# The sample's state updates in a hybrid decoder step: as row tiles of TensorE, four at a time

## The chip, the cores and the metric

The kernel runs on one core of one Trainium2 chip. The metric is the device time of one execution in microseconds; several executions are taken and their median is given. The core has five engines that run side by side, each with its own queue of instructions: TensorE (PE in the profile; its weight loads are PEld), VectorE (DVE), ScalarE (ACT), GpSimd (POOL) and SyncE (SP), which here only issues transfers. Matrix products land in PSUM, of which the kernel uses eight banks of 512 fp32 columns, four in each of the pools `mm` and `gl`; everything else lives in SBUF.

## What is computed

The kernel is one inference step of a two-layer decoder on two groups: a prompt (one sequence of 256 new positions) and a sample (eight sequences with eight new tokens each, which carry a state). Layer 0 mixes tokens by gated linear attention (GLA) with 4 heads, 256 key and 512 value dimensions each; layer 1 is a gMLP. Each layer is followed by a dense MLP of width 8192. All is fp32. The change is in the GLA. For one head, with the running sum b of the log decays:

```python
q_dec = qi * jnp.exp(b); k_inv = ki * jnp.exp(-b); k_to_end = ki * jnp.exp(b_last - b)
scores = jnp.where(causal, jnp.einsum('bhtk,bhsk->bhts', q_dec, k_inv), 0.0)
o = jnp.einsum('bhtk,bhkv->bhtv', q_dec, s) + jnp.einsum('bhts,bhsv->bhtv', scores, vi)
s_new = (jnp.exp(b_last[..., 0, :])[..., None] * s
         + jnp.einsum('bhsk,bhsv->bhkv', k_to_end, vi))
```

For the sample, s is an input of 256x512 for each of 8 sequences and 4 heads, and both o and s_new are needed. The product in s_new contracts over only 8 tokens.

## The kernel before

The 256 prompt positions and the 64 sample tokens stand together as 320 columns. A weight matrix of 2048 rows is read in units of 512 rows by 256 columns (0.5 MB, `unit`, L129). ScalarE rounds a unit to fp32r (`wh`, L144), VectorE takes the rest, which it splits off (`wl`, L145), and TensorE runs three matmuls of 320 columns for each 128x128 piece (`mm3`, L161 to L163), 24 for a unit (two halves of the columns, four pieces of the rows, three each), into PSUM banks of the pool `mm`. Raw weights have three buffers and the split ones four. This makes up nearly all of the time in both layers.

The attention's small work is laid between the units: `Side` (L60) holds a list of steps and gives out about as many after each unit as are left per unit. The steps of a head (`steps`, L629) are spread over the 8 units of its own r projection and the 8 of the next head's k and q projection; the last head has only 8 and 2. Behind that list a scheduler sets the final order on each engine by priority, its own estimate of when operands are ready, and the buffers of the pools. Each engine then works its queue strictly in order.

The steps of a head: the sample's scores, then `sample_first` (L580), which starts the sample's output in one bank `po` of the pool `gl` (four banks); it stays there until the last sample step. Then come five prompt steps (scores, two outputs, two states) with two sample steps after each, and the other sample steps. There are 16 sample steps in a head, one for each of 8 sequences and each half `kt` of the keys (`sample_step`, L589). Each splits 128x512 of the state into `sth` (ScalarE, L597) and `stl` (VectorE, L598), adds two matmuls to `po` (L600), and makes one update matmul (L603) with which VectorE updates the state (L604). After the second half GpSimd's queue stores the sequence's state (L607). States are loaded two sequences ahead (`load`, L577), into four buffers `st` (pool `g3`), which also serve the inputs at the kernel's start.

The eight tokens of a sequence stand in 32 rows: values as high and low part twice (`vts`), keys as high, high, low, low (`kst`, L411 to L416), so that a contraction over 32 rows gives the product of the split parts. Four sequences share the 128 rows of a tile. The update of one of them contracts over all 128 rows, with keys from `kz`, where the other three have zeros in place of keys:

```python
nc.tensor.matmul(pu[:], kz[:, g, i, kt * P : (kt + 1) * P], hd.vts[:, g, :], start=True, stop=True)
nc.vector.scalar_tensor_tensor(st[:, kt, :], st[:, kt, :], hd.dec[...], pu[:], op0=ALU.mult, op1=ALU.add)
```

`kz` is cleared once (L284) and filled by four copies of 32 rows for each half of the keys of a head (L427 to L431).

The prompt's scores (`prompt_scores`, L514) are matmuls with 64 output columns of the array, which TensorE runs in tiles of 128x64, two beside each other.

Of the kernel before, what the change touches and what calls it, by code (L numbers as in the profile page):

```python
# [8 lines left out]
F32 = mybir.dt.float32  # L9
F32R = mybir.dt.float32r  # L10
I32 = mybir.dt.int32
AF = mybir.ActivationFunctionType
ALU = mybir.AluOpType
AX = mybir.AxisListType

P = 128
D = 2048
KT = D // P
TP = 256
DB, DS = 8, 8  # L20
# [3 lines left out]
DK, DV = 256, 512  # L24
CH = 64
NCH = TP // CH
# [51 lines left out]
def step_kernel(ctx: ExitStack, tc: tile.TileContext, A):  # L78
    nc = tc.nc
    uid = [0]  # L80

    def nm(s):
        uid[0] += 1
        return f"{s}_{uid[0]}"
# [16 lines left out]
    def mmtile(n=T):  # L101

        if mx is not None:
            banks[0] = (banks[0] + 1) % 6
        return (mx if banks[0] > 3 else mm).tile([P, n], F32, tag="mm", name=nm("mm"), padded_shape=[P, 512])

    def gltile(n=512):
        return gl.tile([P, n], F32, tag="gl", name=nm("gl"), padded_shape=[P, 512])
# [16 lines left out]
    def col(c):  # L125
        return vec[:, c : c + 1]
# [86 lines left out]
    gst = ExitStack()  # L213
    gp = gst.enter_context(tc.tile_pool(name="gp", bufs=1))
    g2 = gst.enter_context(tc.tile_pool(name="g2", bufs=2))
    g3 = gst.enter_context(tc.tile_pool(name="g3", bufs=4))


    xT = A["xT"].rearrange("(k p) t -> p k t", p=P)
# [59 lines left out]
    fac = gp.tile([P, 2, 9], F32, tag="fac", name="fac")  # L279
    nc.vector.memset(fac[:], 1.0)  # L280


    kz = gp.tile([P, 2, 4, DK], F32R, tag="kz", name="kz")
    nc.gpsimd.memset(kz[:].bitcast(F32), 0.0)  # L284

    glow = gp.tile([96, T], F32R, tag="glow", name="glow")

    wgr = gp.tile([P, 2, TP], F32, tag="sq", name="wgr")[:, 0, :].rearrange("p (k n) -> p k n", n=16)
# [33 lines left out]
    SO = A["o_state_s"]  # L322

    def bc4(ap):

        return ap.rearrange("p (b o t) -> p b o t", b=DB, o=1)

    def chunks(ap):
        return ap.rearrange("p (n w) -> p n w", w=CH)

    class Head:
# [6 lines left out]
        def tiles(hd):  # L338
            hd.qd = gp.tile([P, 2, T], F32, tag="qd", name=nm("qd"))
            hd.qx = gp.tile([P, 2, 5 * CH], F32, tag="qx", name=nm("qx"))  # L340
            hd.kip = gp.tile([P, 2, TP], F32, tag="kip", name=nm("kip"))
            hd.kte = gp.tile([P, 2, T], F32, tag="kte", name=nm("kte"))
            hd.kis = gp.tile([P, 2, DB, 4, DS], F32, tag="kis", name=nm("kis"))
            hd.ktp = gp.tile([P, 2, DK], F32, tag="ktp", name=nm("ktp"))
            hd.vtp = gp.tile([P, 2, DV], F32, tag="vtp", name=nm("vtp"))
            hd.vts = gp.tile([P, 2, DV], F32R, tag="vts", name=nm("vts"))

        def gate_logits(hd):

            hd.dec = g2.tile([P, 2, NCH + DB], F32, tag="dec", name=nm("dec"))  # L350
            for kt in range(2):
                hd.eb[kt] = g2.tile([P, T], F32, tag="eb", name=nm("eb"))
                hd.ei[kt] = g2.tile([P, T], F32, tag="ei", name=nm("ei"))
                f = 2 * hd.h + kt
                ps = gltile(T)
                nc.tensor.matmul(ps[:], wg2[:, f * P : (f + 1) * P], glow[:], start=True, stop=True)
                nc.scalar.activation(hd.eb[kt][:], ps[:], AF.Abs, bias=col(V_BG + f))
                nc.vector.tensor_scalar(hd.ei[kt][:], ps[:], col(V_BG + f), 0.0, op0=ALU.add, op1=ALU.min)
            for kt in range(2):
                nc.scalar.activation(hd.eb[kt][:], hd.eb[kt][:], AF.Exp, scale=-1.0)  # L360
# [38 lines left out]
        def ev_k(hd, kt, ps):  # L399
            ei, ee = hd.ei[kt], hd.ee[kt]  # L400
            kte = hd.kte[:, kt, :]
            nc.vector.tensor_mul(kte, ps[:], ee[:])
            nc.vector.tensor_mul(hd.kip[:, kt, :], ps[:, 0:TP], ei[:, 0:TP])
            nc.vector.tensor_mul(
                hd.kis[:, kt],
                bc4(ps[:, TP:T]).to_broadcast([P, DB, 4, DS]),
                bc4(ei[:, TP:T]).to_broadcast([P, DB, 4, DS]),
            )
            kend = g2.tile([P, TP], F32, tag="vfm", name=nm("kend"))
            nc.vector.tensor_mul(chunks(kend[:]), chunks(kte[:, 0:TP]),  # L410
                                 fac[:, kt, 5:9].unsqueeze(2).to_broadcast([P, NCH, CH]))  # L411
            kst = g2.tile([P, DB, 4, DS], F32, tag="vst", name=nm("kst"))
            two = [P, DB, 2, DS]
            hi = kst[:, :, 0:2, :]
            nc.scalar.copy(hi.bitcast(F32R), bc4(kte[:, TP:T]).to_broadcast(two))
            nc.vector.tensor_sub(kst[:, :, 2:4, :], bc4(kte[:, TP:T]).to_broadcast(two), hi)  # L416
            pt = gltile()
            ks = kst[:].rearrange("p b c t -> p (b c t)")
            for blk in range(2):
                nc.tensor.transpose(pt[:, blk * P : (blk + 1) * P], kend[:, blk * P : (blk + 1) * P], ident[:])  # L420
            for g in range(2):
                nc.tensor.transpose(pt[:, TP + g * P : TP + (g + 1) * P], ks[:, g * P : (g + 1) * P], ident[:])
            cs = slice(kt * P, (kt + 1) * P)
            nc.scalar.copy(hd.ktp[:, :, cs], pt[:, 0:TP].rearrange("p (b f) -> p b f", f=P))
            for i in range(4):
                rows = slice(32 * i, 32 * (i + 1))
                src = pt[rows, TP:].rearrange("p (b f) -> p b f", f=P)  # L427
                if i % 2:
                    nc.scalar.copy(kz[rows, :, i, cs], src)
                else:  # L430
                    nc.vector.tensor_copy(kz[rows, :, i, cs], src)  # L431

        def ev_q(hd, kt, ps):
            qd = hd.qd[:, kt, :]
# [116 lines left out]
                    nc.vector.tensor_add(s1[:, 0:TP], s1[:, 0:TP], sq[:, v, :])  # L551

        def prompt_state(hd, kt):
            if kt == 0:
                hd.S = g3.tile([P, 2, DV], F32, tag="st", name=nm("S"))
            pu = gltile()
            for blk in range(2):
                nc.tensor.matmul(pu[:], hd.ktp[:, blk, kt * P : (kt + 1) * P], hd.vtp[:, blk, :],  # L558
                                 start=(blk == 0), stop=(blk == 1))
            nc.scalar.copy(hd.S[:, kt, :], pu[:])  # L560
            if kt == 1:
                nc.gpsimd.dma_start(A["o_state_p"][hd.h].rearrange("(k p) v -> p k v", p=P), hd.S[:])

        def sample_scores(hd):
            for g in range(2):
# [14 lines left out]
        def sample_first(hd):  # L580

            hd.st = {}
            hd.load(0)
            hd.load(1)
            hd.po = gltile()
            for g in range(2):
                nc.tensor.matmul(hd.po[:], scst[:, g, :], hd.vts[:, g, :], start=(g == 0), stop=False)

        def sample_step(hd, b, kt):  # L589

            g, i = b // 4, b % 4
            if kt == 0 and b + 2 < DB:
                hd.load(b + 2)
            st, po = hd.st[b], hd.po
            sth = g2.tile([P, DV], F32R, tag="sth", name=nm("sth"))
            stl = g2.tile([P, DV], F32R, tag="stl", name=nm("stl"))
            nc.scalar.copy(sth[:], st[:, kt, :])  # L597
            nc.vector.tensor_sub(stl[:], st[:, kt, :], sth[:].bitcast(F32))  # L598
            for part in (stl, sth):
                nc.tensor.matmul(po[:], qm[:, kt, b * P : (b + 1) * P], part[:], start=False,  # L600
                                 stop=(b == DB - 1 and kt == 1 and part is sth))
            pu = gltile()
            nc.tensor.matmul(pu[:], kz[:, g, i, kt * P : (kt + 1) * P], hd.vts[:, g, :], start=True, stop=True)  # L603
            nc.vector.scalar_tensor_tensor(st[:, kt, :], st[:, kt, :], hd.dec[:, kt, NCH + b : NCH + b + 1],  # L604
                                           pu[:], op0=ALU.mult, op1=ALU.add)
            if kt == 1:
                nc.gpsimd.dma_start(SO[b, hd.h].rearrange("(k p) v -> p k v", p=P), st[:])  # L607

        def sample_o(hd):
            h, s1 = hd.h, hd.s1  # L610
# [17 lines left out]

        def steps(hd):  # L629

            yield hd.sample_scores
            yield hd.sample_first
            sample = [lambda b=b, kt=kt: hd.sample_step(b, kt) for b in range(DB) for kt in range(2)]
            prompt = [hd.prompt_scores, lambda: hd.prompt_o(0), lambda: hd.prompt_o(1),
                      lambda: hd.prompt_state(0), lambda: hd.prompt_state(1)]
            for i, p in enumerate(prompt):
                yield p
                yield from sample[2 * i : 2 * i + 2]
            yield from sample[2 * len(prompt) :]
            yield hd.sample_o  # L640
            yield hd.weigh
            yield hd.finish
# [382 lines left out]
    for j in range(KT):  # L1025
        y, g, b = z[:, j, :], col(norm.vg + j), col(norm.vb + j)
# [78 lines left out]
```

## Time and profile before

| | us |
|---|---|
| median of 3 runs (lowest, highest) | 2704.24 (2704.16, 2704.53) |
| the profiled execution, and its span | 2703.75, 2702.0 |
| PE busy | 2692.4 |
| VectorE busy | 1543.5 |
| ScalarE busy | 1182.8 |
| GpSimd busy | 53.5 |
| the 64 update matmuls, L603 (sum of durations) | 23.9 |

How to read it: matmuls overlap in TensorE's pipeline, so the duration of one (0.4 us with 512 columns) is longer than its share of the engine's time. What one costs is the distance from its start to the next one's start. For the same reason PE's busy time says that there is always some matmul under way, not that the stream is at its densest. The GLA's heads lie in the first 460 us; the rest of the span is output projection, MLPs and the second layer, which the change doesn't touch.

### The profile page before, as it was taken

The numbers are of one execution on the slowest core, as the hardware profiler recorded it, in microseconds if no ns is written. First come the engines' busy times: TensorE is split into PE (matmuls) and PEld (weight loads), VectorE is DVE, ScalarE is ACT, GpSimd is POOL, SyncE is SP. The second block draws the span as 40 slices with busy tenths as digits, with TensorE's granted clock in tenths as the row PEclk, the third lists the DMA queues.
The fourth block names the chain that finished last, engine by engine and source line by source line (L and its number), as shares of the span: only waits on it lengthen the run. The fifth ranks groups of instructions, "written<-read, shape, count | busy, mean of one in ns | idle before, by whom it ended". The sixth has DMA issues, their size and how long they took to land.

```text
span 2702.0 us, 44679 instructions
## 1 busy us (share of the span) xinstructions
PE 2692.4 (100%) x18515; PEld 2669.7 (99%) x18515; DVE 1543.5 (57%) x2289; ACT 1182.8 (44%) x1702; POOL 53.5 (2%) x83
## 2 busy tenths in 40 slices
PE   9999999999999999999999999999999999999998
PEld 9999999999999999999999999999999999999998
DVE  6667577885444444444468775587444444444456
ACT  6545455464234334333445554355334323333434
POOL 1000001000000000000001000000000000000000
PEclk9999999999999999999999999999999999999999
DMA  7656556644445455444445444454444545554442
GB/s 243 193 188 228 185 190 218 211 146 156 152 151 154 151 154 151 153 151 153 150 148 171 150 140 136 140 162 155 150 155 150 154 151 153 152 153 152 153 152 79
DMA packets 126396, 434.53 MB, mean 161 GB/s; under 512 B 13680, under 2 KB 17904, under 8 KB 126192
## 3 DMA queue, kind: packets, MB, share of 16 engines
q1 hardware_dynamic: 119136, 407.82, 48.6%
q0 software_dynamic: 6512, 23.20, 2.6%
q8 instruction: 145, 2.38, 0.4%
q10 hardware_dynamic: 544, 0.66, 0.1%
q14 instruction: 59, 0.48, 0.1%
HBM read 409.60 MB, written 22.02 MB: 160 GB/s over the span
## 4 chain that ended last, share of the span: by engine, by line
PE 99%; ACT 0%; DMA 0%; DVE 0%; issue 0%; ACTq 0%; DVEq 0%
PE mm L161 32%; PE mm L163 31%; PE mm L162 31%; PE gl L600 1%; PE gl L603 1%; PE gl L558 1%; PE gl L948 0%; PE gl L542 0%; DMA raw<-gla_w_in 0%; ACT z L1038 0%; PE gl L943 0%; DMA xr<-xT 0%; PE gl L543 0%; PE gl L458 0%; PE gl L456 0%; PE gl L521 0%
## 5 line engine op out<-in xcount | busy, mean ns | idle before, releaser
L145 DVE TENSOR_TENSOR wl<-raw,wh 128x1024 fp32r<-128x1024 f32 (+1 forms) x740 | 901.6, 1219 | 938.8 <-ACT wh L144 936.3
L144 ACT CAST wh<-raw 128x1024 fp32r<-128x1024 f32 (+1 forms) x740 | 771.3, 1044 | 1201.3 <-PE mm L163 1080.9
L163 PE MATMUL mm<-yh,wh 128*128 128x320 f32 x2624 | 805.0, 307 | 0.0
L161 PE MATMUL mm<-yh,wl 128*128 128x320 f32 x2624 | 803.1, 308 | 0.0
L162 PE MATMUL mm<-yl,wh 128*128 128x320 f32 x2624 | 794.2, 303 | 0.0
L161 PE MATMUL mm<-hh,wl 128*128 128x320 f32 x2048 | 630.8, 308 | 0.0
L163 PE MATMUL mm<-hh,wh 128*128 128x320 f32 x2048 | 628.7, 307 | 0.0
L162 PE MATMUL mm<-hl,wh 128*128 128x320 f32 x2048 | 619.6, 303 | 0.0
L162 PEld LDWEIGHTS mm<-yl,wh 128*128 128x128 f32 x2624 | 492.5, 188 | 0.0
L161 PEld LDWEIGHTS mm<-yh,wl 128*128 128x128 f32 x2624 | 490.9, 188 | 0.0
L163 PEld LDWEIGHTS mm<-yh,wh 128*128 128x128 f32 x2624 | 490.8, 187 | 0.0
L162 PEld LDWEIGHTS mm<-hl,wh 128*128 128x128 f32 x2048 | 384.4, 188 | 0.0
L161 PEld LDWEIGHTS mm<-hh,wl 128*128 128x128 f32 x2048 | 384.4, 188 | 0.0
L163 PEld LDWEIGHTS mm<-hh,wh 128*128 128x128 f32 x2048 | 383.0, 187 | 0.0
L161 PE MATMUL mm<-xh,wl 128*128 128x320 f32 x768 | 241.1, 314 | 0.9 <-DVE wl L145 0.5
L163 PE MATMUL mm<-xh,wh 128*128 128x320 f32 x768 | 236.7, 308 | 0.0
L162 PE MATMUL mm<-xl,wh 128*128 128x320 f32 x768 | 234.7, 306 | 0.0
L161 PEld LDWEIGHTS mm<-xh,wl 128*128 128x128 f32 x768 | 144.1, 188 | 5.4 <-issue 1.9
L162 PEld LDWEIGHTS mm<-xl,wh 128*128 128x128 f32 x768 | 144.3, 188 | 3.5 <-issue 1.2
L163 PEld LDWEIGHTS mm<-xh,wh 128*128 128x128 f32 x768 | 143.9, 187 | 1.3
L857 DVE TENSOR_TENSOR hl<-f,hh 128x320 fp32r<-128x320 f32 x128 | 62.3, 489 | 29.4 <-ACT hh L856 29.4
L161 PE MATMUL mm<-oh,wl 128*128 128x320 f32 x256 | 78.1, 309 | 0.6 <-DVE nw L187 0.6
(268 smaller groups left out, 2112.2 us busy)
## 6 DMA issues: line engine op xcount, KB each, us to landing
raw<-mlp_w SPq DMA_DIRECT2D x512, 512.0 KB, 3.5
raw<-gla_w_in SPq DMA_DIRECT2D x94, 512.0 KB, 4.2
raw<-sg_w_in SPq DMA_DIRECT2D x64, 512.0 KB, 3.5
st<-state SPq DMA_DIRECT2D x32, 512.0 KB, 4.3
o_state_s<-st POOLq DMA_DIRECT2D x32, 512.0 KB, 3.8
raw<-gla_w_out SPq DMA_DIRECT2D x32, 512.0 KB, 4.2
raw<-sg_w_out SPq DMA_DIRECT2D x32, 512.0 KB, 3.5
z<-xT POOLq DMA_DIRECT2D x2, 1280.0 KB, 11.6
```

The source lines that it names most:

```text
L144: nc.scalar.copy(hi[:, ks, :], raw[:, ks, :])
L145: nc.vector.tensor_sub(lo[:, ks, :], raw[:, ks, :], hi[:, ks, :].bitcast(F32))
L161: nc.tensor.matmul(ps, wl[:, kk, s], x_h, start=first, stop=False)
L162: nc.tensor.matmul(ps, wh[:, kk, s], x_l, start=False, stop=False)
L163: nc.tensor.matmul(ps, wh[:, kk, s], x_h, start=False, stop=last)
L558: nc.tensor.matmul(pu[:], hd.ktp[:, blk, kt * P : (kt + 1) * P], hd.vtp[:, blk, :], start=(blk == 0), stop=(blk == 1))
L600: nc.tensor.matmul(po[:], qm[:, kt, b * P : (b + 1) * P], part[:], start=False, stop=(b == DB - 1 and kt == 1 and part is sth))
L603: nc.tensor.matmul(pu[:], kz[:, g, i, kt * P : (kt + 1) * P], hd.vts[:, g, :], start=True, stop=True)
L857: nc.vector.tensor_sub(hl[:, j, 0:T], f[:], hh[:, j, 0:T].bitcast(F32))
```

## The change

The padded keys `kz` go. The keys of the sample are kept as they come out of the transposes, 128 rows with four sequences of 32 (`kts`), by one copy on VectorE. The update matmuls are taken out of the sample step into `sample_update`: for four sequences at a time it runs four matmuls, each over 32 rows of keys and values, at four places of 32 rows of the array (the built program gives each of them a tile of 32x128), into four banks. The fourth bank is one of the projections' pool in the first group and one of `gl` in the second. The four state updates of VectorE follow.

The order of the steps is new: scores and start of the output in one step; then the sequences 0 to 3, first halves and update, second halves and update; the five prompt steps; and the sequences 4 to 7 likewise. Five states are loaded at the start of a head, three after the prompt's outputs. There are five buffers for them instead of four. The prompt's state no longer has a buffer there: each half goes into a tile of the head that is free by then (`kip`, `qx`) and is stored by itself.

```diff
-    g3 = gst.enter_context(tc.tile_pool(name="g3", bufs=4))
+    g3 = gst.enter_context(tc.tile_pool(name="g3", bufs=5))
...
-    kz = gp.tile([P, 2, 4, DK], F32R, tag="kz", name="kz")
-    nc.gpsimd.memset(kz[:].bitcast(F32), 0.0)
...
-            for i in range(4):
-                rows = slice(32 * i, 32 * (i + 1))
-                src = pt[rows, TP:].rearrange("p (b f) -> p b f", f=P)
-                if i % 2:
-                    nc.scalar.copy(kz[rows, :, i, cs], src)
-                else:
-                    nc.vector.tensor_copy(kz[rows, :, i, cs], src)
+            nc.vector.tensor_copy(hd.kts[:, :, cs], pt[:, TP:].rearrange("p (b f) -> p b f", f=P))
...
         def prompt_state(hd, kt):
-            if kt == 0:
-                hd.S = g3.tile([P, 2, DV], F32, tag="st", name=nm("S"))
+            S = (hd.qx if kt else hd.kip)[:].rearrange("p a b -> p (a b)")[:, 0:DV]
...
-            nc.scalar.copy(hd.S[:, kt, :], pu[:])
-            if kt == 1:
-                nc.gpsimd.dma_start(A["o_state_p"][hd.h].rearrange("(k p) v -> p k v", p=P), hd.S[:])
+            nc.scalar.copy(S, pu[:])
+            nc.gpsimd.dma_start(A["o_state_p"][hd.h, kt * P : (kt + 1) * P, :], S)
...
-            hd.load(0)
-            hd.load(1)
+            for b in range(5):
+                hd.load(b)
...
         def sample_step(hd, b, kt):
-            g, i = b // 4, b % 4
-            if kt == 0 and b + 2 < DB:
-                hd.load(b + 2)
...
-            pu = gltile()
-            nc.tensor.matmul(pu[:], kz[:, g, i, kt * P : (kt + 1) * P], hd.vts[:, g, :], start=True, stop=True)
-            nc.vector.scalar_tensor_tensor(st[:, kt, :], st[:, kt, :], hd.dec[:, kt, NCH + b : NCH + b + 1],
-                                           pu[:], op0=ALU.mult, op1=ALU.add)
-            if kt == 1:
-                nc.gpsimd.dma_start(SO[b, hd.h].rearrange("(k p) v -> p k v", p=P), st[:])
+        def sample_update(hd, g, kt):
+            pus = [gltile() for _ in range(3)] + [gltile() if g else mmtile(DV)]
+            for i in range(4):
+                rows = slice(32 * i, 32 * (i + 1))
+                nc.tensor.matmul(pus[i][:], hd.kts[rows, g, kt * P : (kt + 1) * P], hd.vts[rows, g, :],
+                                 start=True, stop=True)
+            for i in range(4):
+                b = 4 * g + i
+                st = hd.st[b]
+                nc.vector.scalar_tensor_tensor(st[:, kt, :], st[:, kt, :], hd.dec[:, kt, NCH + b : NCH + b + 1],
+                                               pus[i][:], op0=ALU.mult, op1=ALU.add)
+                if kt == 1:
+                    nc.gpsimd.dma_start(SO[b, hd.h].rearrange("(k p) v -> p k v", p=P), st[:])
+        def sample_rest(hd):
+            for b in range(5, DB):
+                hd.load(b)
...
-            yield hd.sample_scores
-            yield hd.sample_first
...
+            yield lambda: [hd.sample_scores(), hd.sample_first()]
+            for g in range(2):
+                if g:
+                    yield hd.prompt_scores
+                    yield lambda: hd.prompt_o(0)
+                    yield lambda: hd.prompt_o(1)
+                    yield lambda: [hd.sample_rest(), hd.prompt_state(0)]
+                    yield lambda: hd.prompt_state(1)
+                for kt in range(2):
+                    for b in range(4 * g, 4 * g + 3):
+                        yield lambda b=b, kt=kt: hd.sample_step(b, kt)
+                    yield lambda b=4 * g + 3, kt=kt, g=g: [hd.sample_step(b, kt), hd.sample_update(g, kt)]
```

The lines after `sample_step` move by 13 less to 4 more, so L600 becomes L587, L603 becomes L598, L521 and L527 become L512 and L518, and L306 becomes L302. Two numbers change their meaning: L598 was VectorE's split of the state (now L585) and is now the update matmul, and L587 was the start of the sample's output and is now its steps' matmuls.

TensorE, second head, before: the sample's output matmuls (into the bank `gl_2078`) and the update matmuls (from `kz`). Lines of projection matmuls between them are left out.

```order
L600 MATMUL gl_2078<-stl_2132,qm 128x512
L600 MATMUL gl_2078<-sth_2131,qm 128x512
L603 MATMUL gl_2137<-vts_1691,kz 128x512
...
L600 MATMUL gl_2078<-stl_2171,qm 128x512
L600 MATMUL gl_2078<-sth_2170,qm 128x512
L603 MATMUL gl_2176<-vts_1691,kz 128x512
```

TensorE, second head, now: the first update of the first block (four matmuls, the fourth into `mm_2162`), and the first update of the second block (three, and one later).

```order
L587 MATMUL gl_2072<-stl_2112,qm 128x512
L587 MATMUL gl_2072<-sth_2111,qm 128x512
...
L598 MATMUL gl_2159<-vts_1684,kts_1685 128x512
L598 MATMUL gl_2160<-vts_1684,kts_1685 128x512
L598 MATMUL gl_2161<-vts_1684,kts_1685 128x512
L598 MATMUL mm_2162<-vts_1684,kts_1685 128x512
...
L598 MATMUL gl_2588<-vts_1684,kts_1685 128x512
L598 MATMUL gl_2589<-vts_1684,kts_1685 128x512
L598 MATMUL gl_2590<-vts_1684,kts_1685 128x512
...
L598 MATMUL gl_2591<-vts_1684,kts_1685 128x512
```

Each sample step had its update beside it; now the updates of four steps follow the steps, four together in the first block, and in the second three together and the fourth 25 matmuls later. Heads 1 and 3 read the same.

TensorE, last head, before: the block of the prompt's scores (into `gl_4377`), which the sample's output steps (into `gl_4374`) follow.

```order
L521 MATMUL gl_4377<-qd_3980,kip_3982 64x64
L527 MATMUL gl_4377<-qx_3981,kte_3983 64x192
...
L527 MATMUL gl_4377<-qd_3980,kte_3983 64x64
...
L600 MATMUL gl_4374<-stl_4428,qm 128x512
L600 MATMUL gl_4374<-sth_4427,qm 128x512
```

TensorE, last head, now: three of the single updates, and the block of scores (into `gl_4527`), with a sample step's two matmuls inside it.

```order
L598 MATMUL gl_4481<-vts_3970,kts_3971 128x512
...
L598 MATMUL gl_4482<-vts_3970,kts_3971 128x512
...
L598 MATMUL gl_4483<-vts_3970,kts_3971 128x512
...
L518 MATMUL gl_4527<-qx_3964,kte_3966 64x192
...
L587 MATMUL gl_4358<-stl_4464,qm 128x512
L587 MATMUL gl_4358<-sth_4463,qm 128x512
L518 MATMUL gl_4527<-qx_3964,kte_3966 64x128
```

In this head the 16 updates stand as 8 single ones, two groups of three and one of two, and the scores' block is cut once.

VectorE, at the start of the kernel, before: `xl` are the low parts of the input, `wl_244` those of the third weight unit, `wgp` a tile of the gate's weights.

```order
L231 TENSOR_TENSOR xl_90<-xr_234,xh_89 128x640
L267 CAST mask_s<-ms_115 128x32
L231 TENSOR_TENSOR xl_90<-xr_236,xh_89 128x640
L145 TENSOR_TENSOR wl_244<-raw_242,wh_243 128x1024
L231 TENSOR_TENSOR xl_90<-xr_302,xh_89 128x640
L306 MEMSET wgp_418 128x1024
```

VectorE, at the start of the kernel, now (`wl_242` is the third unit's part):

```order
L231 TENSOR_TENSOR xl_90<-xr_232,xh_89 128x640
L231 TENSOR_TENSOR xl_90<-xr_234,xh_89 128x640
L302 MEMSET wgp_416 128x1024
L145 TENSOR_TENSOR wl_242<-raw_240,wh_241 128x1024
L231 TENSOR_TENSOR xl_90<-xr_300,xh_89 128x640
```

The memset of `wgp` stood behind the third unit's split and one input's; now it stands ahead of both.

## Rows read from the trace of the kernel before

**Rows 1.** The page: engines' busy time with share and instructions, granted clock by slice.

```profile
PE 2692.4 (100%) x18515; PEld 2669.7 (99%) x18515; DVE 1543.5 (57%) x2289; ACT 1182.8 (44%) x1702; POOL 53.5 (2%) x83
...
PEclk9999999999999999999999999999999999999999
```

**Rows 2.** The page: chain that ended last, by engine and by line.

```profile
PE 99%; ACT 0%; DMA 0%; DVE 0%; issue 0%; ACTq 0%; DVEq 0%
PE mm L161 32%; PE mm L163 31%; PE mm L162 31%; PE gl L600 1%; PE gl L603 1%; PE gl L558 1%; PE gl L948 0%; PE gl L542 0%; DMA raw<-gla_w_in 0%; ACT z L1038 0%; PE gl L943 0%; DMA xr<-xT 0%; PE gl L543 0%; PE gl L458 0%; PE gl L456 0%; PE gl L521 0%
```

**Rows 3.** Waits: us in total, times, longest.

```profile
ACT wh L144 <- PE mm L163: 1080.9, 487, 3.1
...
DVE st L604 <- PE gl L603: 34.5, 17, 3.4
```

**Rows 4.** Timeline of PE, third head: start us, duration us.

```profile
297.06 0.39 PE L600 MATMUL gl<-sth,qm 128*128 128x512 f32 x1
297.29 0.40 PE L603 MATMUL gl<-vts,kz 128*128 128x512 f32 x1
297.53 0.31 PE L163 MATMUL mm<-xh,wh 128*128 128x320 f32 x1
...
297.97 0.31 PE L163 MATMUL mm<-xh,wh 128*128 128x320 f32 x1
```

**Rows 5.** Timeline of PE where the first head's prompt scores begin.

```profile
78.94 0.63 PE L587 MATMUL gl<-vts,scst 128*128 128x512 f32 x2
79.50 0.28 PE L521 MATMUL gl<-qd,kip 128*64 128x64 f32 x2
```

**Rows 6.** Line L521: duration ns min/median/max, weight loads and matmuls.

```profile
L521 PEld LDWEIGHTS gl<-qd,kip x64: 132/136/138, 79.5 to 404.4; 128*64 128x64 f32 x64
L521 PE MATMUL gl<-qd,kip x64: 219/222/271, 79.5 to 404.5; 128*64 128x64 f32 x64
```

**Rows 7.** Timeline where the first head's prompt scores end, PE and its weight loads.

```profile
80.78 0.28 PE L527 MATMUL gl<-qd,kte 128*64 128x64 f32 x2
...
80.99 0.19 PEld L600 LDWEIGHTS gl<-stl,qm 128*128 128x128 f32 x1
80.99 0.50 PE L600 MATMUL gl<-stl,qm 128*128 128x512 f32 x1
81.10 0.19 PEld L600 LDWEIGHTS gl<-sth,qm 128*128 128x128 f32 x1
```

**Rows 8.** Timeline of weight loads where the scores begin.

```profile
79.50 0.15 PEld L521 LDWEIGHTS gl<-qd,kip 128*64 128x64 f32 x2 [0.37 <-issue]
```

**Rows 9.** Timeline of VectorE at the start, with idle time before and releaser.

```profile
10.25 0.19 DVE L265 TENSOR_TENSOR ms<-ms,ms 128x32 f32<-128x32 f32 x1 [0.29 <-POOL ms L262]
...
14.36 0.91 DVE L306 MEMSET wgp<- 128x1024 f32 x1 [0.28 <-DVE xl L231]
```

**Rows 10.** Timeline of PE at the start, third unit.

```profile
13.40 0.41 PE L161 MATMUL mm<-xh,wl 128*128 128x320 f32 x1 [0.48 <-DVE wl L145]
```

**Rows 11.** Timeline of GpSimd at the start.

```profile
5.29 1.82 POOL L284 MEMSET kz<- 128x2048 f32 x1
```

**Rows 12.** Line L431: duration ns min/median/max.

```profile
L431 DVE CAST kz<-gl x16: 402/416/423, 71.6 to 374.7; 32x256 fp32r<-32x256 f32 x16
```

**Rows 13.** Windows of first and last head: us, then PE, PEld, DVE, ACT, POOL busy.

```profile
79.00:113.00 34.00, 34.00 (x219) 30.31 (x218) 20.57 (x29) 16.71 (x25) 2.94 (x4) 1.00 0.61 186
...
400.00:452.00 52.00, 52.00 (x329) 47.26 (x328) 37.38 (x57) 27.83 (x47) 6.54 (x9) 1.00 0.64 213
```

**Rows 14.** DMA issues: KB each, median us to landing.

```profile
st<-state SPq DMA_DIRECT2D x32, 512.0 KB, 4.3
o_state_s<-st POOLq DMA_DIRECT2D x32, 512.0 KB, 3.8
```

**Rows 15.** VectorE's groups by form: busy us, mean ns, idle us before.

```profile
L145 DVE TENSOR_TENSOR wl<-raw,wh 128x1024 fp32r<-128x1024 f32 x734 | 898.7, 1225 | 935.7 <-ACT wh L144 933.3
L604 DVE SCALAR_TENSOR_TENSOR st<-st,dec,gl 128x512 f32<-128x512 f32 x64 | 46.2, 742 | 34.6 <-PE gl L603 34.5
```

More of the change, by code (lines that the diff above doesn't have):

```diff
@@ L346, in tiles @@
             hd.vts = gp.tile([P, 2, DV], F32R, tag="vts", name=nm("vts"))
+            hd.kts = gp.tile([P, 2, DK], F32R, tag="kts", name=nm("kts"))
         def gate_logits(hd):
@@ L629, in steps @@
         def steps(hd):
-            yield hd.sample_scores
-            yield hd.sample_first
[L633 to L639, printed above, removed]
+            yield lambda: [hd.sample_scores(), hd.sample_first()]
[10 more added lines that the diff above has]
+                    yield lambda b=4 * g + 3, kt=kt, g=g: [hd.sample_step(b, kt), hd.sample_update(g, kt)]
             yield hd.sample_o
```

## The prediction

> **What bounds the kernel now.** I read the engines' totals first: TensorE (PE) is busy for 2692.4 of 2702.0 us, at a granted clock that stays full (2.4 GHz) in all 40 slices [rows 1]. The chain of waits says the same: 99% of it is PE, nearly all in the three projection matmuls of `mm3` [rows 2]. The reader is to see that nothing else ends last. The waits by engine show who is ahead of whom: ScalarE waits 1080.9 us in 487 places for PE to free a weight buffer, and VectorE 34.5 us for PE's state updates [rows 3]. So a microsecond counts only if PE's own stream grows or shrinks, or if PE begins to wait.
>
> **The update matmuls.** Before, 64 update matmuls (L603) run between the others at one spacing: one starts at 297.29, the next matmul at 297.53, and the one ahead of it at 297.06 [rows 4]. That is 0.23 us each, 14.7 us in all, wholly on the path. After, the same 64 run as 32-row tiles. If four ran in the time of one and nothing else changed, 11 us would go. That is the most that can.
>
> But a 32-row tile is another shape of the array, and the trace shows what a change of shape costs. The prompt's scores (L521, L527) run in tiles of 128x64. Before them, two matmuls of 512 columns begin at 78.94 and fill 0.63 us [rows 5], at 0.39 us each [rows 4], so the second begins at 79.18 and the next would follow at 79.41. The first score matmul begins at 79.50 and lasts 0.27 us where 0.22 is the median [rows 6]: its weights, too, load only then (0.05). **Change in: 0.14 us.** At the other end the last pair begins at 80.78 and fills 0.28 us, so its second begins at 80.84 and a next would be due some 0.06 later, at 80.90. The sample's matmul begins at 80.99 and lasts 0.50 instead of 0.39 us, because its weights load uncovered: the following load can start only at 81.10 [rows 7]. It starts in effect at 81.10. **Change back: 0.20 us.**
>
> The Trainium skill has this as a rule ("TensorEngine Tiling (Array Packing)", Key Properties: changing the tiling mode, not just the tile, drains TensorE), and these rows agree; if it did not hold for row tiles, the sum would be rival B's.
>
> For tiles of 32x128 I take the same two changes. One thing differs: the first load has 128 weight columns, not 64, and takes 0.11 us (80.99 to 81.10) instead of 0.05, so the change in costs 0.20. Inside a group I take it that tiles load and run side by side: two score tiles load within 0.15 us together [rows 8], though each load lasts 0.13 to 0.14 [rows 6], so a next one comes 0.01 later. No row shows four row tiles; the bounds are below.
>
> A group of n then costs 0.20 + 0.23 + 0.20 + 0.01(n-1) us, against 0.23n before: four gain 0.26, three gain 0.04, two lose 0.18, and a single one loses 0.40.
>
> How many groups there are decides, and the order of instructions says it. One PSUM buffer of four holds the sample's output all through a head. In the first block the fourth update goes into a projection's bank, and the four stand together. In the second it needs a buffer that VectorE must free first, so three stand together and the fourth alone, 25 matmuls later. Heads 1 to 3 have two of each per head: 6 fours, 6 threes, 6 singles. In the last head, which has fewer weight units to spread over, the order has 8 singles, 2 threes and one pair. So: 6 x 0.26 + 8 x 0.04 - 1 x 0.18 - 14 x 0.40 = 1.56 + 0.32 - 0.18 - 5.60 = **3.9 us lost**. In the last head a sample step also stands inside the score tiles, one more change in and back: 0.14 + 0.20 = **0.3 us lost**.
>
> **The start.** The fifth state buffer serves the input loads too, and with it VectorE's order changes: a memset of 0.91 us now stands ahead of the third weight unit's split [rows 9]. PE already waits there, 0.48 us [rows 10]. Against that, the key memset of 1.82 us is gone from GpSimd [rows 11], so the 0.29 us that VectorE waited for the masks [rows 9] go. 0.91 - 0.29 = **0.6 us lost**. Bounds: 0.48 gained, if the memset finds a gap and the wait goes; 0.91 lost.
>
> **Edits at nothing.** Each key tile had four copies of 32 rows, two on ScalarE and two on VectorE, these of 0.42 us [rows 12]; now one on VectorE of about one such copy. Both engines have room: VectorE is busy 20.6 of 34 us in a head, ScalarE 16.7 [rows 13]. Uncovered, it could cost or give 8 x 0.4 = 3 us at most, and nothing waited for it but ScalarE's own next copy. The prompt's state leaves in two halves, from tiles that the next head overwrites a whole block of samples later. The five loads go out earlier. The three later ones wait for stores of updated states: 3.8 us to land, 4.3 to load [rows 14], then two passes over 128x512 to split, each about as long as the update's 0.74 [rows 15]: 9.6 us. In between, heads 1 to 3 have 10.6 us of projection matmuls (72 at 0.147, [rows 4]) and the scores' 1.5 us (79.50 to 80.99, [rows 7, 8]), and the prompt's outputs and state besides. Behind these loads on SP's queue stand weight loads, for which PE would wait if they came late; but ScalarE's wait for free weight buffers [rows 3] says that weights lie ready. If that cover went, the price is a load's 4.3 us for each late block.
>
> **Sum.** 3.9 + 0.3 + 0.6 = 4.8 us. On the profiled execution's own 2703.75 us (span 2702.0, the rest around it) that makes 2708.6; it lies 0.5 below the median of the runs, 2704.24, so the forecast is **2709 us**. A run of this kernel can be told from no change from about 0.2%, 5.4 us: the forecast lies just inside.
>
> **Rivals.**
> B, row tiles need no change of shape. For it: no row shows a row tile. Against it: both ends of all the score blocks. Then a group of n costs 0.23 + 0.01(n-1): 6 x 0.66 + 8 x 0.44 + 0.22 = 7.7 us gained, 0.6 lost at the start: 7.1 off 2704.2, **2697**, faster. It decides from about half the change's cost downwards. The Trainium skill measures 3.07 times for four row tiles of 512 columns ("TensorE: Matmul & The Clock Gate", Part 3); by that the six fours alone would gain 6 x 0.92 x (1 - 1/3.07) = 3.7 us, an estimate from that page.
>
> C, the four loads follow each other, 0.11 us each. For it: nothing shows more than two side by side. Each tile after the first costs 0.10 more: 18 + 16 + 1 = 35 of them, 3.5 us: **2712.5**, slower.
>
> D, the tiles do not run side by side at all. 35 x 0.22 = 7.7 us more: **2717**.
>
> E, PE waits at the fourth update. VectorE frees the buffer with an update of 0.74 us [rows 15], and now does four in a row, 3 us. For it: VectorE is busy 37.4 of 52 us in the last head [rows 13], and it takes its work in order. Against it: 25 matmuls, 3.8 us, stand between. It decides once VectorE is more than 3 us behind there. Late by one weight split of 1.23 us [rows 15] at 8 such places: 10 us more, **2719**.
>
> F, a change costs half for row tiles: singles lose 0.2, fours gain 0.46, threes 0.24: 2.8 + 1.9 - 2.8 = 1.9 gained, 0.15 lost at the cut and 0.6 at the start: **2703**, no change.
>
> **Chances.** Forecast 0.47 (2706 to 2712, a little more of it below the bound than above), B 0.17, C 0.14, F 0.11, E 0.07, D 0.04. Faster takes B and a little of F: 0.20. Within 0.2%: 0.25 of the forecast and the rest of F, 0.33. Slower: 0.22 of the forecast, C, D and E, 0.47. The range runs from B to D, 2697 to 2717; the forecast's own is 2706 to 2712.
>
> **What would show it.** Right: in the new update line, fours whose matmuls start within 0.05 us of each other, a gap of some 0.1 us ahead of each group in which nothing loads, and after it a projection matmul that lasts 0.1 us longer than its kind; a single update taking 0.6 us out of the stream; PE's wait at the third weight unit near 1 us. Wrong: updates at the usual 0.23 us spacing with loads ahead of time (B), starts 0.1 us (C) or 0.2 us (D) apart, or PE idle before an update with VectorE as the releaser (E).

## The result, and the profile after

The changed kernel takes **2708.82 us** (median of 22 runs), the kernel before in the same session 2704.3 us. The ratio is 1.0017, with a 95% interval of 1.0011 to 1.0023: slower by some 4.5 us, by less than the 0.2% that the prediction took for the bound of what can be told. The forecast was 2709 us. The profiled executions differ by as much: a span of 2706.3 us instead of 2702.0.

The page's totals, PE and its weight loads first, read as in [rows 1]:

```profile
PE 2696.1 (100%) x18515; PEld 2662.9 (98%) x18515; DVE 1540.1 (57%) x2281; ACT 1178.0 (44%) x1686; POOL 53.1 (2%) x86
```

PE is still the bound, with the same number of instructions, and is now busy longer while its weight loads are busy less: around a group they stand still twice, and inside it they run beside each other, as the rows below show. The timeline of PE around the first group of four (start us, duration us):

```profile
82.90 0.31 PE L163 MATMUL mm<-xh,wh 128*128 128x320 f32 x1
83.14 0.50 PE L598 MATMUL gl<-vts,kts 32*128 32x512 f32 x3
83.15 0.50 PE L598 MATMUL mm<-vts,kts 32*128 32x512 f32 x1
83.57 0.42 PE L161 MATMUL mm<-xh,wl 128*128 128x320 f32 x1
83.83 0.32 PE L162 MATMUL mm<-xl,wh 128*128 128x320 f32 x1
```

The same stretch of its weight loads:

```profile
82.76 0.19 PEld L163 LDWEIGHTS mm<-xh,wh 128*128 128x128 f32 x1
83.14 0.19 PEld L598 LDWEIGHTS gl<-vts,kts 32*128 32x128 f32 x3 [0.19 <-issue]
83.14 0.18 PEld L598 LDWEIGHTS mm<-vts,kts 32*128 32x128 f32 x1
83.57 0.19 PEld L161 LDWEIGHTS mm<-xh,wl 128*128 128x128 f32 x1 [0.24 <-issue]
83.68 0.19 PEld L162 LDWEIGHTS mm<-xl,wh 128*128 128x128 f32 x1
```

This answers to [rows 5 to 8]. The projection matmul at 82.90 is followed after 0.24 instead of 0.146 us. The four start within 0.01 us of each other, with their loads, ahead of which no load ran for 0.19 us. The next projection matmul starts 0.42 us later and loads only then, after another 0.24 us without a load, and its successor comes 0.26 instead of 0.146 us behind it. From 82.90 to 83.83 are 0.93 us, of which the two projection matmuls account for 0.29: the group of four costs **0.64 us**. Now a single update:

```profile
129.29 0.31 PE L162 MATMUL mm<-xl,wh 128*128 128x320 f32 x1
129.53 0.50 PE L598 MATMUL gl<-vts,kts 32*128 32x512 f32 x1
129.96 0.42 PE L163 MATMUL mm<-xh,wh 128*128 128x320 f32 x1
130.22 0.31 PE L161 MATMUL mm<-xh,wl 128*128 128x320 f32 x1
```

From 129.29 to 130.22 are again 0.93 us: alone, an update costs the same. In this way all 29 groups give 0.62 us for a single one, 0.65 for the pair, 0.64 for threes and fours (medians), 18.3 us in all. The 64 updates before, measured likewise, took 0.237 us each, 15.2 us.

What PE waited for (us in total, times, longest):

```profile
PE gl L152 <- DVE ones L116: 1.1, 1, 1.1
PE mm L161 <- DVE nw L187: 1.0, 1, 1.0
PE mm L161 <- DVE wl L145: 0.9, 2, 0.6
```

The first row is the kernel's very start, the same before. The second is the end of the last head (0.6 us before), the third the first weight units. None is at an update.

### The profile page after: what moved, and what is told of

Read it like the earlier page. It is cut to its first block, busy times and chain, and to the rows that moved or that the text cites. A ratio compares the mean times of both kernels' runs of the same rounds, so it can differ in the third digit from the quotient of the medians.

```text
span 2706.3 us, 44638 instructions
## 1 busy us (share of the span) xinstructions
PE 2696.1 (100%) x18515; PEld 2662.9 (98%) x18515; DVE 1540.1 (57%) x2281; ACT 1178.0 (44%) x1686; POOL 53.1 (2%) x86
## 4 chain that ended last, share of the span: by engine, by line
PE 99%; ACT 0%; DVE 0%; DMA 0%; issue 0%; SPq 0%; ACTq 0%; DVEq 0%
PE mm L161 32%; PE mm L163 31%; PE mm L162 31%; PE gl L587 1%; PE gl L549 1%; PE gl L598 0%; PE gl L955 0%; PE gl L533 0%; DMA xr<-xT 0%; ACT z L1045 0%; PE gl L950 0%; PE gl L534 0%; PE gl L449 0%; PE gl L447 0%; PE gl L559 0%; PE gl L512 0%
```

## The experiments

**All rows for each update.** The row tiles are undone, the order and the buffers stay.

```diff
-                rows = slice(32 * i, 32 * (i + 1))
-                nc.tensor.matmul(pus[i][:], hd.kts[rows, g, kt * P : (kt + 1) * P], hd.vts[rows, g, :],
+                nc.tensor.matmul(pus[i][:], hd.kts[:, g, kt * P : (kt + 1) * P], hd.vts[:, g, :],
```

> The changed kernel with each update matmul over all 128 rows of keys and values, as one full tile, and all else as it is (each state then gets the product of all four sequences' keys, which changes the state outputs, not the number or length of instructions). Theory (a group of row tiles pays 0.40 us for two changes of the array's shape, so 29 groups cost 18.3 us where 64 full matmuls cost 64 x 0.2375 = 15.2): 3.1 us faster than the changed kernel, 2705.7 us, and no gap ahead of the updates. Rival (the loss comes from the new order and the five buffers, not from the shape): as the changed kernel, 2708.8 us.

Measured: 2705.18 us, 1.0004 times before (0.9995 to 1.0013), span 2703.0. The timeline of PE at the same place:

```profile
83.01 0.31 PE L163 MATMUL mm<-xh,wh 128*128 128x320 f32 x1
83.16 0.86 PE L597 MATMUL gl<-vts,kts 128*128 128x512 f32 x3
83.86 0.40 PE L597 MATMUL mm<-vts,kts 128*128 128x512 f32 x1
84.09 0.31 PE L161 MATMUL mm<-xh,wl 128*128 128x320 f32 x1
```

The four fill 0.93 us (83.16 to 84.09), with no gap ahead of them or behind. Of the 4.3 us that the change costs in its profile, 3.3 are the shape; the new order and buffers account for about 1. The medians' intervals (this one and the changed kernel's) still touch, so the weight is on the traces.

**Row tiles alone.** The kernel before, with each step's own update as a row tile; the copies that filled `kz` fill `kts` instead, and `kz` and its memset are gone.

```diff
...
-            nc.tensor.matmul(pu[:], kz[:, g, i, kt * P : (kt + 1) * P], hd.vts[:, g, :], start=True, stop=True)
+            rows = slice(32 * i, 32 * (i + 1))
+            nc.tensor.matmul(pu[:], hd.kts[rows, g, kt * P : (kt + 1) * P], hd.vts[rows, g, :], start=True, stop=True)
```

> The kernel before with one part of the change: each sample step's own update as one 32-row tile with the unpadded keys, in the order of before, four buffers, no padded keys. The order has 30 places with one update and 17 with two, 15 of these two on the same rows. Theory (0.40 us for each place, 0.23 for each pass): 30 x 0.63 + 15 x 0.86 + 2 x 0.64 = 33.1 us in place of 15.2, 17.9 us slower than before, 2722 us. Rival (a change of shape is paid only where the neighbours wait, or is half as dear as read from the scores): 8.5 us slower or less, under 2713 us. Rival (the cost is in the new order): as before, 2704 us.

Measured: 2721.32 us, 1.0062 times before (1.0049 to 1.0076), 17.3 us more. The forecast was 17.9. A place with two on the same rows:

```profile
90.53 0.40 PE L599 MATMUL gl<-sth,qm 128*128 128x512 f32 x1
90.85 0.73 PE L603 MATMUL gl<-vts,kts 32*128 32x512 f32 x2
91.51 0.42 PE L161 MATMUL mm<-xh,wl 128*128 128x320 f32 x1
91.76 0.40 PE L599 MATMUL gl<-stl,qm 128*128 128x512 f32 x1
```

From 90.53 to 91.76 are 1.23 us, less 0.225 and 0.145 for the neighbours: 0.86 us for two passes, 0.22 more than for one. So the cost goes with the number of places where the shape changes, and the rivals with half a price or none fall.

**Every group twice.**

```diff
-            for i in range(4):
+            for i in [0, 1, 2, 3] * 2:
                 rows = slice(32 * i, 32 * (i + 1))
```

> The changed kernel with every group of update matmuls run twice over, into the same banks with the same result, all else as it is: doubles what is done in the row tiles and leaves the number of changes of shape at 29. Theory (0.63 us of a group are 0.40 of change and 0.22 of work, and the second pass's weights load under the first): 29 x 0.22 = 6.4 us slower than the changed kernel, 2715.2 us. Rival (row tiles work slowly, 0.5 us for 512 columns as their durations say, and no change is paid): 29 x 0.5 = 14.5 us slower, 2723 us.

Measured: 2714.69 us, 1.0038 times before (1.0025 to 1.0052), 5.9 us above the changed kernel. The forecast was 6.4.

```profile
83.00 0.31 PE L163 MATMUL mm<-xh,wh 128*128 128x320 f32 x1
83.24 0.50 PE L598 MATMUL gl<-vts,kts 32*128 32x512 f32 x3
83.25 0.49 PE L598 MATMUL mm<-vts,kts 32*128 32x512 f32 x1
83.58 0.40 PE L598 MATMUL gl<-vts,kts 32*128 32x512 f32 x3
83.58 0.39 PE L598 MATMUL mm<-vts,kts 32*128 32x512 f32 x1
83.91 0.42 PE L161 MATMUL mm<-xh,wl 128*128 128x320 f32 x1
84.16 0.31 PE L162 MATMUL mm<-xl,wh 128*128 128x320 f32 x1
```

From 83.00 to 84.16 are 1.16 us, so 0.87 for two passes of four: the second adds 0.23. Inside, four tiles do take the time of one, and 0.40 of a group's 0.64 us are the two changes. The second pass lasts 0.39 to 0.40 us a matmul, as a full one does: the first's 0.50 holds its uncovered load. The total alone would not settle it: here PE also waited 0.9 us for VectorE, at three single updates, and 1.4 us less than in the changed kernel at the start and at the end of the last head. The weight is on the spacing above.

**Fours only.** One element is written into each of the four banks ahead of a group, and the group's first matmul waits for all four; the other three are issued behind it.

```diff
-            pus = [gltile() for _ in range(3)] + [gltile() if g else mmtile(DV)]
+            pus = [gltile() for _ in range(3)] + [mmtile(DV)]
+            gates = [nc.vector.memset(pus[i][0:1, 0:1], 0.0) for i in range(4)]
...
+                    for gt in gates:
...
+                        tc.add_manual_dep(first, gt.name, mybir.DependencyInfo(
+                            mybir.DependencyClass.Sync, mybir.DependencyReason.DATA), reason="bank free")
```

> The changed kernel with all 64 updates in 16 groups of four: the fourth bank is always one of the projections', and VectorE writes one element into each of the four banks before the first matmul of a group, which waits for all four writes. Theory (the number of groups decides, 0.64 us for a group of any size): 29 x 0.63 = 18.3 us become 16 x 0.638 = 10.2 us, 8.1 us faster than the changed kernel, 2700.7 us, which is faster than before too. Rival (the single updates were the price of not waiting for VectorE's free banks; in fours PE waits instead): waits of 0.5 us at 10 to 16 groups give 5 to 8 us back, 2706 to 2709 us, with VectorE as PE's releaser ahead of the updates.

Measured: 2705.6 us, 1.0004 times before (0.9995 to 1.0013): 3 us less than the changed kernel instead of 8. The 16 groups stand as meant and cost 16 x 0.637 = 10.2 us. No update waits. But PE waits elsewhere, and more is lost behind the wait; PE at the end of the last head:

```profile
461.36 0.31 PE L163 MATMUL mm<-oh,wh 128*128 128x320 f32 x1
464.49 0.41 PE L161 MATMUL mm<-oh,wl 128*128 128x320 f32 x1 [2.81 <-DVE nw L187]
...
466.10 0.47 PE L162 MATMUL mm<-ol,wh 128*128 128x320 f32 x1
466.36 0.47 PE L163 MATMUL mm<-oh,wh 128*128 128x320 f32 x1
```

Windows of the same place (columns as in [rows 13], PEclk third from the end):

```profile
464.60:466.00 1.40, 1.40 (x10) 1.40 (x11) 0.85 (x2) 0.69 (x1) 0.00 (x0) 0.98 1.03 296
466.10:469.20 3.10, 3.10 (x13) 3.10 (x13) 2.48 (x3) 2.04 (x3) 0.00 (x0) 0.50 0.66 218
469.40:473.00 3.60, 3.60 (x27) 3.60 (x26) 3.60 (x8) 2.68 (x6) 1.15 (x2) 1.00 0.79 248
```

The wait grew by 1.85 us over the changed kernel's. After it, 12 matmuls run at a granted clock of 0.50 (1.2 GHz), 0.267 us apart instead of 0.146, another 1.45 us. So 3.3 us were lost there. Some 2 us more went in small gaps before that, the largest in sample steps that wait for VectorE.

**Fours in heads 1 to 3.** The same code under `if hd.h < H - 1`, the last head as in the changed kernel.

> Fours with gates as in fours_only, but in heads 1 to 3 alone; the last head has its updates as the changed kernel has them (8 singles, 2 threes, a pair). Theory A (each group saved is worth 0.63 us; what fours_only fell short of was lost at the end of the last head, where PE waited 2.8 us in one place): in heads 1 to 3 18 groups become 12, 3.8 us less than the changed kernel, 2705.0 us, and the wait at the end stays near the changed kernel's 1.0 us. Rival B (the gates cost in every head, by sample steps that wait for VectorE): about 2 us of that are given back, 2707 us, with the wait at the end as in the changed kernel.

Measured: 2706.09 us, 1.0007 times before (0.9998 to 1.0016), between A and B. The wait at the end is 1.0 us, as A has it. B's price is there too, but smaller, in one sample step per head:

```profile
127.58 0.31 PE L161 MATMUL mm<-xh,wl 128*128 128x320 f32 x1
127.95 0.19 PEld L587 LDWEIGHTS gl<-stl,qm 128*128 128x128 f32 x1 [0.32 <-DVE stl L585]
127.95 0.50 PE L587 MATMUL gl<-stl,qm 128*128 128x512 f32 x1
128.29 0.40 PE L587 MATMUL gl<-sth,qm 128*128 128x512 f32 x1
```

The step's load waits for VectorE's split of the state (`stl`). From 127.58 to 128.29 are 0.71 us; the same step takes 0.47 in the changed kernel (127.71 to 128.18), 0.24 less. Three heads make 0.7 us of the 1.1 by which A is missed; the rest is not placed.

**Another bank for the last norm.** In fours_only:

```diff
-            pr = gltile(T)
+            pr = mmtile() if h == H - 1 else gltile(T)
```

> fours_only with one line changed: in the last head the sums of squares for the samples' norm go into a bank of the projections' pool, not of the attention's. Theory A (the wait of 2.8 us for VectorE's norm operation is for a bank: the output projection takes over the attention's banks, and the last of them is read until that operation ends): the wait goes, 2.8 us less than fours_only, 2702.8 us, faster than before. Rival C (the wait is for a weight split that stands behind the norm operation on VectorE, so the bank doesn't matter): as fours_only, 2705.6 us, with the wait still there.

Measured: 2702.76 us, 0.9996 times before (0.9987 to 1.0005). The forecast was 2702.8. PE's waits:

```profile
PE gl L628 <- ACT os L625: 1.1, 1, 1.1
PE gl L152 <- DVE ones L116: 1.1, 1, 1.1
PE mm L161 <- ACT xh L230: 0.5, 1, 0.5
PE mm L161 <- DVE wl L145: 0.3, 1, 0.3
```

The wait for the norm operation is gone, and with it the stretch at half clock; a new wait of 1.1 us, for a copy of the sample's output, stands in the last head. The wait was for a bank. The timeline of fours_only says so too: VectorE's splits around the norm operation end at 463.70 and begin again at 466.39, so that PE, which went on at 464.49, can't have waited for one behind it (rival C). That the number was met to 0.04 us is luck: theory A counted the wait's 2.8 us alone, the clock's 1.45 us went as well, and some 1.4 us came back, 1.1 of them in the new wait.

**The same line in the kernel before.**

> The kernel before with that one line alone. Theory A: PE's wait of 0.6 us for the norm operation goes, 2703.5 us at best, 0.03% less. Rival C: no change, 2704.1 us.

Measured: 2708.11 us, 1.0016 times before (1.0007 to 1.0025). Neither theory has this. The wait for the norm operation went, as A says, but the matmul that fills the bank now stands earlier in PE's queue and waits for its own input:

```profile
PE mm L625 <- DVE s L622: 2.9, 1, 2.9
```

Windows behind it:

```profile
457.00:461.00 4.00, 4.00 (x19) 4.00 (x18) 3.93 (x9) 2.52 (x3) 0.00 (x0) 0.57 0.32 125
```

Again a wait of 2.9 us is followed by a stretch at the lower clock.

**The memsets to GpSimd.** fours_other_bank with

```diff
-            nc.vector.memset(t[:].bitcast(F32), 0.0)
+            nc.gpsimd.memset(t[:].bitcast(F32), 0.0)
```

> fours_other_bank, and the two memsets of the gate's weight tiles moved from VectorE to GpSimd, which takes them from ahead of VectorE's third and fourth weight splits. Theory A with the start as forecast (the memset ahead of the third split costs 0.4 to 0.6 us): 2702.8 - 0.5 = 2702.3 us. Rival (PE's wait for the third split is set by the inputs and masks ahead of it, or GpSimd's memsets come late for the gate's weights): 2702.8 us or more.

Measured: 2702.43 us, 0.9995 times before (0.9986 to 1.0004). VectorE at the start:

```profile
9.93 1.54 DVE L231 TENSOR_TENSOR xl<-xr,xh 128x640 fp32r<-128x640 f32 x2
12.22 1.23 DVE L145 TENSOR_TENSOR wl<-raw,wh 128x1024 fp32r<-128x1024 f32 x1 [0.74 <-ACT wh L144]
```

The third split now waits for ScalarE's half of it instead of standing behind a memset, and PE loses 0.2 us there (matmuls of the unit before and this one start at 13.15 and 13.50) instead of 0.5 in fours_other_bank. The two medians, 0.33 us apart, don't tell theory A from the rival, since their runs overlap; the trace bears A out at the third split. It is the shortest version, 6.4 us under the changed kernel, but its interval takes in no change against before.

## Why the prediction was right, point by point

**The mechanism and the size of a group.** The prediction read 0.14 us in and 0.20 back from the ends of the score blocks [rows 5 to 8], raised the way in to 0.20 for the longer weight load, and carried both over to row tiles, which no row showed. A group then takes 0.63 to 0.66 us whatever its size; 0.62 to 0.65 were measured. The Trainium skill's rule that a change of tiling mode drains TensorE ("TensorEngine Tiling (Array Packing)", Key Properties) agrees, and is now seen on a second shape. Rivals B, C, D and F fall by the timeline of the four: the change is paid in full, and the tiles load and run side by side.

The Trainium skill's 3.07 times for four row tiles ("TensorE: Matmul & The Clock Gate", Part 3) lies between two numbers here: without a change, as in the second pass of "twice", four updates take 0.23 instead of 0.95 us, 4 times as fast; with both changes 0.64 instead of 0.95, 1.5 times.

**The number of groups.** The order gave 6 fours, 8 threes, a pair and 14 singles, and the trace has them. The 14 singles lose 14 x (0.62 - 0.237) = 5.4 us, the fours gain 1.9 and the threes 0.6, and the pair loses 0.2: 3.1 us lost. The forecast was 3.9. Some 0.45 us of the difference are the updates before, sized at 0.230 from one place: with its neighbours one took 0.237. The rest are groups 0.01 to 0.02 us cheaper than forecast. Heads 1 to 3, with 6 fours, 6 threes and 6 singles, come out even; the 3.1 us are lost in the last head, where 8 updates stand alone.

**The cut in the scores.** Forecast 0.3; in the last head the block is left, the sample step's two matmuls run, and the block is entered again:

```profile
417.48 0.49 PE L518 MATMUL gl<-qx,kte 128*64 128x192 f32 x2
417.90 0.50 PE L587 MATMUL gl<-stl,qm 128*128 128x512 f32 x1
418.23 0.39 PE L587 MATMUL gl<-sth,qm 128*128 128x512 f32 x1
418.55 0.32 PE L518 MATMUL gl<-qx,kte 128*64 128x128 f32 x1
```

The two start 0.33 us apart and the scores come 0.32 behind, against 0.225 each: 0.20 us, and the change ahead of 417.90 adds 0.16: 0.37 by the starts in nanoseconds.

**The start.** 0.6 forecast, 0.4 measured, but by luck, for the mechanism was another. The prediction had PE's wait at the third unit near 1 us. It fell from 0.48 us [rows 10] to 0.35:

```profile
13.16 0.31 PE L163 MATMUL mm<-xh,wh 128*128 128x320 f32 x1
13.81 0.41 PE L161 MATMUL mm<-xh,wl 128*128 128x320 f32 x1 [0.35 <-DVE wl L145]
```

PE came to it 0.55 us later (its matmul ahead of the wait started at 12.61 before), and so met the split sooner. The memset does hold the third split up, as the last experiment shows, by some 0.3 us for PE. Most of the 0.55 us went at one place in the first unit, where a matmul and its weight load wait for an input's low part (`xl`); on VectorE the cast of a mask stands ahead of that part:

```profile
7.43 0.38 DVE L255 CAST mask_p<-mf 128x384 int32<-128x384 f32 x1
8.27 0.19 PEld L162 LDWEIGHTS mm<-xl,wh 128*128 128x128 f32 x1 [0.39 <-DVE xl L231]
```

Before, that cast stood at 9.58, behind these parts, and no load waited there. "Row tiles alone" has the cast at the same place and the same wait (0.38 us at 8.28), with four buffers and no memset ahead of the third split; what it shares with the change at the start is that `kz` and its memset are gone. So the term that the prediction booked as 0.29 us gained (masks that come sooner) cost some 0.4. Single profiled executions differ here, too: in the kernel before with the other bank, where VectorE's order at the start is as before, PE comes out of the third unit's wait at 13.64 instead of 13.40.

**What the sum left out.** Once in each of heads 1 to 3 the kernel before lost 0.25 us at a sample step that waited for VectorE (127.97 to 128.60 in the first, where 0.38 are due); 0.09 us are left of it (127.71 to 128.18), so 0.5 us were gained. And PE's wait at the end of the last head grew by 0.4. So 3.1 + 0.4 + 0.4 - 0.5 + 0.4 = 3.8 us of the 4.3 by which the spans differ; the other 0.5 us are not placed. The mechanism of the main term was right; that the sum of 4.8 came so near is in part luck, because errors of both signs are in it.

**Rival E** did not happen at an update, in this kernel or in fours; in "twice" three single updates did wait for VectorE, 0.3 us each instead of the 1.23 that E assumed. In fours PE waited for VectorE at another place: VectorE's operation on the last head's norm (`nw`, L187) reads a bank that PE's next projection needs. E's own time, 2719 us, lay outside the range that the prediction gave its rivals, 2697 to 2717.

## What to carry to other kernels

A matmul in another tile shape costs its work and a fixed price for the way there and back, here 0.40 us, as much as 1.7 of the matmuls it replaces: count the uninterrupted groups in the order that is built, not the matmuls, and pack only where a group replaces enough of them (here three to break even). A group that needs several free buffers at once falls apart under a scheduler that issues each matmul as its own buffer comes free, unless something makes the first wait for all. A gain inside a stage can be lost again at its end, where PE waits for another engine: in fours 3.3 of 8.1 us went to a longer wait for a bank at the end, and to the clock after it.

## What the runs showed of the hardware that was not expected

After PE had stood for about 3 us (2.8 us at 461, 2.9 us in the kernel before with the other bank), the granted clock fell to the lower level, not at once but 1.6 and 1.1 us after work had begun again, and stayed there for 3.2 us. Twelve matmuls of 320 columns then took 0.267 us each instead of 0.146. After the waits of 0.6 and 1.0 us at the same place no spacing shows it. In fours this added 1.45 us to the wait's own time.

The first matmul in a new shape shows a duration 0.10 us longer than its kind (0.50 instead of 0.40), and so does the first one after the return (0.42 instead of 0.31). In a list of durations that marks a change of shape only where PE didn't wait: a matmul behind a wait, without any change of shape, is as long (0.41 at 464.49 in fours, 0.50 at 127.95 in the fours of heads 1 to 3).
